# Conv state, conv weights and last conv inputs moved by rows and turned on chip, and w_out's split tied behind the newest scores

## The chip, the core and the metric

The kernel runs on one core of a Trainium2 chip. A core has TensorE (PE in the profile; PEld is its weight load), VectorE (DVE), ScalarE (ACT), GpSimd (POOL) and SyncE (SP), each with a queue of its own that it works through in order. In this kernel SP issues all transfers; they run on 16 DMA engines. The metric is the device time of one execution in microseconds (us), the median of several runs.

## The reference

One step of a one-layer streaming encoder, in float32. For the prompt (2048 tokens of 1024) and a sample of 32 tokens:

```
u  = rmsnorm(h, g_pre_mix);  z = u @ w_in      # columns B | C | X | Q | K | V, 512 each
zp = concat(hist, C * X)                       # hist: 0 for the prompt, state_conv for the sample
y  = b_conv + sum(zp[:, j:j+t] * w_conv[j] for j in 0..2);   conv_out = zp[:, -2:]
a  = differential attention of 4 heads on Q, K, V (two softmax maps, chunk mask, rmsnorm with g_subln)
h  = h + rmsnorm(concat(B * y, a) @ w_out)
h  = h + rmsnorm(relu(rmsnorm(h) @ w_up)^2 @ w_down)
h  = h + rmsnorm((p @ w_pe) * sigmoid(h @ w_g))
```

It returns h, k and v of both parts, and `conv_out` of both, the last two columns of C * X: `conv_prompt` and `conv_sample`, 2 x 512 values each. `state_conv` is 2 x 512, `w_conv` 3 x 512, `b_conv` 512, `g_subln` 128.

## The kernel before

All matrix products run on PE in float16 pairs: a float32 operand is split into a high half (ACT, L170) and a low half (DVE, L105) by `split`, and three products are added. Features lie on the 128 partitions in the conv and the projections, so the 512 conv channels are 4 groups (j, one for each head) of 128 partitions.

Start (L740 to L852, about 0 to 85 us). SP loads the x tiles, the gain and the first weight tiles of w_in. `hist` (state_conv) is loaded behind x tile 1 (L744), `wcv`, `bcv` and `gsa` (w_conv, b_conv, g_subln) in `small_loads` (L757 to L759); each reads a vector of DRAM into 128 partitions, so that one packet carries one value. The order of PE, ACT and DVE is written out by hand here (`manual_schedule`, L782): x tile 0 is normed and turned, `warm(11)` puts 11 matmuls on PE, then the second weight tile is prepared and the first projections run.

Attention part (about 85 to 945 us). For each head j a unit is 128 queries: `scores` (L596) puts matmuls on PE and, for each 512 columns, one DVE step (L610) that adds the bias and takes the running maximum; POOL negates the maximum (L100), ACT takes the exponential (L617). `turn` and `values` follow for the units before it. Between these steps `weave` (L1066) puts pieces of a second list of work, `between(j)` (L1029): the projections of the next head, and the conv of this one as three chunks, C, X and B. `c_group` (L429) evacuates C into `cz`, one buffer of 2 + 2048 columns, whose first two are 0 (in `czs`, for the sample, they are a POOL copy of `hist`, L434). `x_group` multiplies X into it. `b_group` (L446) forms y on POOL and DVE, multiplies with B and stores it to `mixc_d` (L461); on the sample's turn it stores the last two columns of `cz` and `czs` to the outputs (L463, L464), one pair for each head, one value in each packet. The buffer of y (tag kvo, three of them) is shared with the k and v outputs. The buffer of `cz` is taken over by `sample_attention` (L513). Each weight tile of w_in takes five steps: load (L256), maximum on DVE (L140), two small steps through PE, split.

In head 3 `w_out_load` (L875) loads the eight row blocks of w_out and takes their maxima (L891), `w_out_scales` makes the scales, and from unit 9 on the second list is `early` (L1018): `w_out_split` (L917) splits the eight blocks, one for each step of the list, and `mix_tile` runs the first two tiles of the output projection. From about 945 us on follow the output projection, the MLP and the gate, bound by PE.

Outside `manual_schedule` a planner puts each engine's instructions in order when the kernel is built: it runs its own estimate of the time, and an instruction that is ready goes ahead of earlier ones that aren't. `issue_after(ins)` makes the planner keep each instruction of a block that runs on the engine of `ins` behind `ins`.

Of the kernel before, what the change touches and what calls it, by code (L numbers as in the profile page):

```python
# [9 lines left out]
F32 = mybir.dt.float32  # L10
# [7 lines left out]
P = 128  # L18
D = 1024
FT = D // P  # L20
S = 2048
NTG = 4
TG = 512
NH = 4
DS = 32
# [4 lines left out]
BIG = 3.0e38  # L30
# [4 lines left out]
def hymba_step_kernel(  # L35
# [192 lines left out]
    mconv = cst.tile([P, NH * (NTG + 1)], F32, name="mconv")  # L228
    nlam = cst.tile([P, 1], F32, name="nlam")
    alam = cst.tile([P, 1], F32, name="alam")  # L230
    wcv = cst.tile([P, 3, NH], F32, name="wcv")
    bcv = cst.tile([P, NH], F32, name="bcv")
    hist = cst.tile([P, 2, NH], F32, name="hist")
    gsa = cst.tile([P, 1], F32, name="gsa")
    gain = {}

# [209 lines left out]
    def b_group(c, tg, parts=1):  # L446
        j = c.j
        n = TG if tg < NTG else DS
        z = cz[0][:, tg * TG:tg * TG + TG + 2] if tg < NTG else cz[1]
        yt = misc.tile([P, TG], F32, tag="kvo", bufs=3, name="yt")  # L450
        y = yt[:, :n]
        ts(G, y, z[:, 0:n], wcv[:, 0, j:j + 1], MUL, bcv[:, j:j + 1], ADD)
        stt(y, z[:, 1:n + 1], wcv[:, 1, j:j + 1], y, MUL, ADD)
        stt(y, z[:, 2:n + 2], wcv[:, 2, j:j + 1], y, MUL, ADD)
        ps = yield from proj_fm(c.w, tg, parts)
        o = y if tg < NTG else mix_s[:, j, :]
        stt(o, ps, c.iw, y, MUL, MUL)
        k = j * (NTG + 1) + tg
        V.tensor_reduce(out=mconv[:, k:k + 1], in_=o, op=MAX, axis=AX.X, apply_absolute_value=True)
        if tg < NTG:  # L460
            st(out=mixc_d[j, :, cols(tg)], in_=o)  # L461
        else:
            st(out=conv_prompt[0, 0][:, j * P:(j + 1) * P].rearrange("w p -> p w"), in_=cz[0][:, S:S + 2])  # L463
            st(out=conv_sample[0, 0][:, j * P:(j + 1) * P].rearrange("w p -> p w"), in_=cz[1][:, DS:DS + 2])  # L464

    GROUP = {GK: k_group, GV: v_group, GC: c_group, GX: x_group, GB: b_group}

# [114 lines left out]
    class Unit:  # L582
# [13 lines left out]
        def scores(self):  # L596
            h, nk, qb = heads[self.j], self.nk, self.qb
            qs, q = h[("qs", qb // 4)], slice(qb % 4 * P, (qb % 4 + 1) * P)
            self.s, self.z = [], []
            for m in range(2):  # L600
                s_ = att.tile([P, S], F32, tag="s", bufs=4, name=f"s{m}")
                prev = None
                for c0, w_ in self.chunks:
                    ps = psc.tile([P, TG], F32, tag="sc", bufs=3, name="sc")
                    kc = h["ks"][m][:, c0:c0 + w_]
                    T.matmul(ps[:, :w_], qs[:, 2 * m, q], kc, start=True, stop=False)
                    T.matmul(ps[:, :w_], qs[:, 2 * m + 1, q], kc, start=False, stop=True)  # L607
                    mx = t1("mx")
                    b0 = S - nk + c0
                    V.tensor_tensor_reduce(out=s_[:, c0:c0 + w_], in0=ps[:, :w_], in1=bias[:, b0:b0 + w_],  # L610
                                           scale=h["idd"], scalar=-BIG if prev is None else prev,
                                           op0=ADD, op1=MAX, accum_out=mx)
                    prev = mx
                    if c0 + w_ == nk:
                        nm, zz = t1("nm"), t1(f"z{m}")
                        ts(G, nm, prev, -1.0, MUL)
                        A.activation(out=s_[:, :nk], in_=s_[:, :nk], func=AF.Exp, bias=nm, accum_out=zz)  # L617
                        self.s.append(s_)
                        self.z.append(zz)
                    yield  # L620
# [88 lines left out]
    with tc.tile_pool(name="p1", bufs=1, side="right") as p1:  # L709
# [30 lines left out]
        ld(out=g1, in_=g_pre_mix[0].partition_broadcast(P))  # L740
        order[1].step()
        loaded += [load_x(1)]
        for w in range(2):
            ld(out=hist[:, w, :], in_=state_conv[0, 0][w].rearrange("(t p) -> p t", p=P))  # L744
        loaded += [load_x(t) for t in range(2, 7)]

        def small_loads():
            ldx = ld
            lam = []
            for i, (a_, b_) in enumerate(((lambda_q1, lambda_k1), (lambda_q2, lambda_k2))):  # L750
                la = p1.tile([P, 64], F32, tag=f"la{i}", name="la")
                lb = p1.tile([P, 64], F32, tag=f"lb{i}", name="lb")
                ldx(out=la, in_=a_[0].partition_broadcast(P))
                ldx(out=lb, in_=b_[0].partition_broadcast(P))
                lam.append((la, lb))
            for w in range(3):
                ldx(out=wcv[:, w, :], in_=w_conv[0][w].rearrange("(t p) -> p t", p=P))  # L757
            ldx(out=bcv, in_=b_conv[0].rearrange("(t p) -> p t", p=P))
            ldx(out=gsa, in_=g_subln[0].rearrange("(p o) -> p o", o=1))  # L759
            yield  # L760
            le = []
            for la, lb in lam:
                V.tensor_tensor(out=la, in0=la, in1=lb, op=MUL)
                sm_, ex = t1("lsum"), t1("lexp")
                V.tensor_reduce(out=sm_, in_=la, op=ADD, axis=AX.X)
                A.activation(out=ex, in_=sm_, func=AF.Exp)
                le.append(ex)
            V.tensor_tensor(out=nlam, in0=le[1], in1=le[0], op=SUB)
            ts(V, nlam, nlam, -0.2, ADD)
            absval(alam, nlam)  # L770

            ts(V, gsa, gsa, 0.8, MUL)
            gs, _, sa, gain["isa"] = scaled_gain(p1, g_subln[0], "g3", 10)
            gain["sa"] = sa
            ts(V, gsa, gsa, sa, MUL)
# [6 lines left out]
        with tc.manual_schedule(engines={ET.PE, ET.Activation, ET.DVE}):  # L782
            first, second = order[0], order[1]

            def summed(t):
                rs[t] = sum_x(*loaded[t])

            def normed(t):
                norm_x(*loaded[t], rs[t])

            def turned(t):
                turn_x(t, *loaded[t])

            def warm(n):

                for _ in range(n):
                    T.matmul(smb[:, :P], ident, ident, start=True, stop=True)

            warm(12)
            summed(0)  # L800
            first.step()
            first.step()
            normed(0)
            first.step()
            summed(1)
            norm_by_pool(loaded[1][0], rs[1])
            _, gain["su"], gain["isu"] = gain_scale(g1, "g1", 9)
            first.step()
            turned(0)
            warm(11)  # L810
            second.step()
            summed(2)
            groups = [c_group(first, 0, 4), x_group(second, 0, 4)]
            next(groups[0])
            second.step()
            normed(2)
            second.step()
            turned(1)
            second.step()
            nxt["k"] = 2  # L820
            summed(3)
            next(groups[0])
            next(groups[1])
            turned(2)
            normed(3)
            next(groups[1])
            summed(4)
            for t in range(2, NT):

                if len(loaded) < NT:  # L830
                    loaded.append(load_x(len(loaded)))
                if t + 2 < NT:
                    normed(t + 2)
                if t + 1 < NT:
                    turned(t + 1)
                if t + 3 < NT:
                    summed(t + 3)
                if t % 4 == 0:
                    groups = [g(c, t // 4, 4 if t < S // P else 1) for g, c in ((c_group, first), (x_group, second))]
                for g in groups:  # L840
                    next(g, None)
                if t % 4 == 3 or t == NT - 1:
                    for g in groups:
                        all_of(g)
                if t in (2, 6):
                    next(later, None)
                if 5 < t < 14:
                    prepare(3)
                if t >= 14 and order[4].done < 4:
                    prepare(4)  # L850
# [66 lines left out]
    def w_out_split():  # L917

        s_put.close()
        here["small2"] = ctx.enter_context(tc.tile_pool(name="sml2", bufs=4, reuse_waits="tile"))  # L920
        pwo = s_wo.enter_context(tc.tile_pool(name="pwo", bufs=1, reuse_waits="tile"))
        here["ppost"] = s_wo.enter_context(tc.tile_pool(name="ppost", bufs=1, reuse_waits="tile"))
        for r in ROWS:
            w = wo[r] = pwo.tile([P, 2, D], F16, tag="w", bufs=8, name="w")
            split(w[:, 0], w[:, 1], out_scale["sgs"][r], out_scale["aswo" if r < 4 else "swo"])
            yield


# [907 lines left out]
```

## Time and profile before

| | us |
|---|---|
| median of 3 runs (2559.03 to 2565.12) | 2562.55 |
| the profiled execution | 2561.83 |
| its span, first to last instruction | 2560.1 |
| PE busy in the span | 2464.4 (96%) |
| DVE, ACT, POOL busy | 1691.2, 1138.2, 747.8 |
| mean granted clock of TensorE | 0.986 of full speed |
| elements stored by L463 and L464, to landing | 9.9 in the middle |

The page divides the span into busy time of each engine. Busy time alone doesn't say what a change is worth; that is read from the views of single stretches: an engine's timeline (when each instruction started, how long it took, how long the engine stood idle before it and for what), the view of who waited for whom, windows with the busy time of every engine, and the list of transfers with their time from issue to landing. TensorE's granted clock is 1.00 at 2.4 GHz and 0.50 at 1.2 GHz; a value between them is a mean over a stretch.

### The profile page before, as it was taken

How to read it: one execution, taken by the hardware profiler on the slowest of the kernel's cores; microseconds unless marked ns; L12 is line 12 of the kernel's file. 1: busy time of each engine (PE TensorE's matmuls, PEld its weight loads, DVE VectorE, ACT ScalarE, POOL GpSimd, SP SyncE). 2: the span in 40 equal slices, each digit the busy share in tenths (PEclk: the TensorE clock that was granted, in tenths of full speed). 3: DMA queues.
4: the chain of work that ended last, by engine and by line, in shares of the span. 5: the costliest groups of instructions: out<-in, count | busy, mean ns of one | idle time of the engine just before them, and what ended most of it. 6: DMA issues, size and time to landing. Idle time of an engine off the chain costs nothing.

```text
span 2560.1 us, 41714 instructions
## 1 busy us (share of the span) xinstructions
PE 2464.4 (96%) x15979; PEld 1286.8 (50%) x15979; DVE 1691.2 (66%) x2930; ACT 1138.2 (44%) x1976; POOL 747.8 (29%) x1299
## 2 busy tenths in 40 slices
PE   8999999998999789999999999999999999999998
PEld 7756654754754445444444444444444444444444
DVE  6578968957988857865656656645455447645664
ACT  5436635634653645544434434444233322424553
POOL 2143344333333333423223222210121102323442
PEclk9999999999999799999999999999999999999999
DMA  5134534523553334554454454366554547531221
GB/s 179 51 83 95 109 68 93 118 50 85 120 113 83 88 122 154 179 214 153 153 181 156 149 181 141 136 228 231 185 203 140 177 155 240 202 108 59 79 83 54
DMA packets 350489, 345.35 MB, mean 135 GB/s; under 512 B 155920, under 2 KB 246448, under 8 KB 350288
## 3 DMA queue, kind: packets, MB, share of 16 engines
q1 hardware_dynamic: 350288, 342.68, 44.5%
q8 instruction: 125, 2.05, 0.3%
q14 instruction: 76, 0.62, 0.1%
HBM read 206.68 MB, written 97.92 MB: 119 GB/s over the span
## 4 chain that ended last, share of the span: by engine, by line
PE 64%; DVE 5%; DMA 3%; issue 2%; POOL 1%; ACT 1%; DVEq 0%; SPq 0%; POOLq 0%; ACTq 0%
PE mm L1368 8%; PE mm L1370 7%; PE mm L1369 7%; PE mm L1599 6%; PE mm L1601 6%; PE mm L1600 6%; PE mm L944 5%; PE mm L946 5%; PE mm L948 5%; DVE s L105 1%; PE lin L313 1%; PE lin L314 1%; PE lin L315 1%; DVE s L610 1%; PE ptr L185 1%
## 5 line engine op out<-in xcount | busy, mean ns | idle before, releaser
L1601 PE MATMUL mm<-v,hl 128*128 128x512 f16 x896 | 341.0, 381 | 4.4 <-DVE hl L1561 4.3
L1599 PE MATMUL mm<-v,hl 128*128 128x512 f16 x896 | 340.8, 381 | 3.8 <-ACT hl L1560 3.4
L1600 PE MATMUL mm<-v,hl 128*128 128x512 f16 x896 | 341.4, 381 | 0.0
L313 PE MATMUL lin<-uh,whl 128*128 128x512 f16 (+1 forms) x832 | 264.4, 333 | 16.9 <-DVE yt L105 14.0
L314 PE MATMUL lin<-ul,whl 128*128 128x512 f16 (+1 forms) x832 | 264.9, 333 | 1.4 <-DVE ul L105 1.3
L315 PE MATMUL lin<-uh,whl 128*128 128x512 f16 (+1 forms) x832 | 264.3, 333 | 0.2 <-DVE whl L105 0.2
L1561 DVE TENSOR_TENSOR hl<-fr,hl 128x1024 f16<-128x1024 f32 x112 | 147.5, 1326 | 174.4 <-ACT hl L1560 171.7
L1560 ACT ACTIVATE hl<-fr 128x1024 f16<-128x1024 f32 x112 | 116.9, 1051 | 303.7 <-PE mm L1601 290.5
L617 ACT ACTIVATE s<-s,nm 128x128 f32<-128x128 f32 (+15 forms) x128 | 153.6, 1200 | 167.9 <-POOL nm L100 167.3
L1368 PE MATMUL mm<-u,w 128*128 128x512 f16 x448 | 169.8, 379 | 1.1 <-ACT w L170 1.1
L1369 PE MATMUL mm<-u,w 128*128 128x512 f16 x448 | 169.8, 379 | 0.0
L1369 PE MATMUL mm<-u2b,w 128*128 128x512 f16 x448 | 169.8, 379 | 0.0
L1368 PE MATMUL mm<-u2b,w 128*128 128x512 f16 x448 | 169.2, 380 | 0.1
L1370 PE MATMUL mm<-u,w 128*128 128x512 f16 x448 | 168.9, 379 | 0.0
L1370 PE MATMUL mm<-u2b,w 128*128 128x512 f16 x448 | 168.5, 379 | 0.0
L1599 PEld LDWEIGHTS <-hl 128*128 128x128 f16 x896 | 88.0, 98 | 114.1 <-issue 7.7
L610 DVE CUSTOM_DVE_ANT_0 s<-sc,bias,mx 128x512 f32<-128x512 f32 (+3 forms) x192 | 134.9, 702 | 15.1 <-PE sc L607 10.5
L1601 PEld LDWEIGHTS <-hl 128*128 128x128 f16 x896 | 87.9, 98 | 113.2 <-DVE hl L1561 7.2
L1600 PEld LDWEIGHTS <-hl 128*128 128x128 f16 x896 | 88.0, 98 | 105.2 <-issue 2.6
L1370 PEld LDWEIGHTS <-w 128*128 128x128 f16 x896 | 87.6, 98 | 105.3
L1368 PEld LDWEIGHTS <-w 128*128 128x128 f16 x896 | 88.7, 99 | 100.2 <-ACT w L170 1.2
L1369 PEld LDWEIGHTS <-w 128*128 128x128 f16 x896 | 87.6, 98 | 98.7 <-issue 0.3
(456 smaller groups left out, 5844.4 us busy)
## 6 DMA issues: line engine op xcount, KB each, us to landing
ff_d<-e SPq DMA_DIRECT2D x224, 256.0 KB, 2.1
fr<-ff_d SPq DMA_DIRECT2D x112, 512.0 KB, 4.4
raw<-in_w_down_dram SPq DMA_DIRECT2D x80, 512.0 KB, 4.7
xt<-in_x_prompt_dram SPq DMA_DIRECT2D x32, 512.0 KB, 4.4
stg<-in_w_up_dram SPq DMA_DIRECT2D x16, 1024.0 KB, 6.5
stgd<-in_w_down_dram SPq DMA_DIRECT2D x16, 1024.0 KB, 5.4
stg<-in_w_in_dram SPq DMA_DIRECT2D x24, 512.0 KB, 3.9
h_d<-ht SPq DMA_DIRECT2D x16, 512.0 KB, 2.9
```

The lines of the kernel that those rows point to most:

```text
L313: T.matmul(o, w[:, 0, ft], rh[:, ft, c], start=(ft == 0), stop=False)
L314: T.matmul(o, w[:, 0, ft], rl[:, ft, c], start=False, stop=False)
L315: T.matmul(o, w[:, 1, ft], rh[:, ft, c], start=False, stop=(ft == FT - 1))
L610: V.tensor_tensor_reduce(out=s_[:, c0:c0 + w_], in0=ps[:, :w_], in1=bias[:, b0:b0 + w_], scale=h["idd"], scalar=-BIG if prev is None else ...
L617: A.activation(out=s_[:, :nk], in_=s_[:, :nk], func=AF.Exp, bias=nm, accum_out=zz)
L1368: T.matmul(o, w[:, c, 0, kt], x[:, :, 0, kt], start=first and kt == 0, stop=False, skip_group_check=True)
L1369: T.matmul(o, w[:, c, 0, kt], x[:, :, 1, kt], start=False, stop=False, skip_group_check=True)
L1370: T.matmul(o, w[:, c, 1, kt], x[:, :, 0, kt], start=False, stop=kt == 3, skip_group_check=True)
L1561: V.tensor_tensor(out=hl[:, 1], in0=fr, in1=hl[:, 0], op=SUB)
L1599: T.matmul(ps, hl[:, 0, u % 2, c], v[:, 0], start=(u == 0), stop=False)
L1600: T.matmul(ps, hl[:, 0, u % 2, c], v[:, 1], start=False, stop=False)
L1601: T.matmul(ps, hl[:, 1, u % 2, c], v[:, 0], start=False, stop=(u == NU - 1))
```

## The change

The 25 rows of 128 values that the conv and the norm need (8 of state_conv, 12 of w_conv, 4 of b_conv, 1 of g_subln) are loaded as rows into one tile `rows_` behind x tile 1. After `warm(11)` one PE transpose turns it, and a DVE copy puts it into `few`; `hist`, `wcv` and `bcv` are views of `few`, and `gsa` is made from its last column. The loads in `small_loads` are gone.

In each head two POOL copies put the last two columns of `cz` and `czs` into `ends`. In head 3 one PE transpose turns `ends` (16 columns) into 16 rows, ACT copies them out of PSUM, and two stores write 8 rows of 512 B each.

`scores` notes its newest DVE step in `here["ev"]`, and each block's split in `w_out_split` is put behind it by `issue_after`; as that step is DVE's, it binds the low half and not ACT's high half.

```diff
+    few = cst.tile([P, 25], F32, name="few")
+    hist = few[:, 0:8].rearrange("p (w t) -> p w t", t=NH)
+    wcv = few[:, 8:20].rearrange("p (w t) -> p w t", t=NH)
+    bcv = few[:, 20:24]
+    ends = cst.tile([P, 2, 2, NH], F32, name="ends")
...
-            st(out=conv_prompt[0, 0][:, j * P:(j + 1) * P].rearrange("w p -> p w"), in_=cz[0][:, S:S + 2])
-            st(out=conv_sample[0, 0][:, j * P:(j + 1) * P].rearrange("w p -> p w"), in_=cz[1][:, DS:DS + 2])
+            G.tensor_copy(ends[:, 0, :, j], cz[0][:, S:S + 2])
+            G.tensor_copy(ends[:, 1, :, j], cz[1][:, DS:DS + 2])
+            if j == NH - 1:
+                pt = ptp.tile([P, TG], F32, tag="tp", name="pte")
+                T.transpose(pt[:16, :P], ends.rearrange("p a w t -> p (a w t)"), ident)
+                eo = misc.tile([P, TG], F32, tag="kvo", bufs=3, name="eo")
+                A.copy(eo[:16, :P], pt[:16, :P])
+                for a_, o_ in ((0, conv_prompt), (8, conv_sample)):
+                    st(out=o_[0, 0].rearrange("w (t p) -> (w t) p", p=P), in_=eo[a_:a_ + 8, :P])
...
+                    here["ev"] = getattr(ev, "ins", ev)
...
-        for w in range(2):
-            ld(out=hist[:, w, :], in_=state_conv[0, 0][w].rearrange("(t p) -> p t", p=P))
+        rows_ = p1.tile([25, P], F32, name="rows")
+        for a_, n_, i_ in ((0, 8, state_conv[0, 0]), (8, 20, w_conv[0])):
+            ld(out=rows_[a_:n_], in_=i_.rearrange("w (t p) -> (w t) p", p=P))
+        ld(out=rows_[20:24], in_=b_conv[0].rearrange("(t p) -> t p", p=P))
+        ld(out=rows_[24:25], in_=g_subln[0].rearrange("(o p) -> o p", o=1))
...
-            for w in range(3):
-                ldx(out=wcv[:, w, :], in_=w_conv[0][w].rearrange("(t p) -> p t", p=P))
-            ldx(out=bcv, in_=b_conv[0].rearrange("(t p) -> p t", p=P))
-            ldx(out=gsa, in_=g_subln[0].rearrange("(p o) -> p o", o=1))
...
-            ts(V, gsa, gsa, 0.8, MUL)
+            ts(V, gsa, few[:, 24:25], 0.8, MUL)
...
             warm(11)
+            pt = ptp.tile([P, TG], F32, tag="tp", name="ptf")
+            T.transpose(pt[:, :25], rows_, ident[:25, :25])
+            V.tensor_copy(few, pt[:, :25])
             second.step()
...
-            split(w[:, 0], w[:, 1], out_scale["sgs"][r], out_scale["aswo" if r < 4 else "swo"])
+            with tc.issue_after(here["ev"]):
+                split(w[:, 0], w[:, 1], out_scale["sgs"][r], out_scale["aswo" if r < 4 else "swo"])
```

## Rows read from the trace of the kernel before

**Rows 1.** The page: busy us of PE in the span.
```profile
PE 2464.4 (96%) x15979; PEld 1286.8 (50%) x15979; DVE 1691.2 (66%) x2930; ACT 1138.2 (44%) x1976; POOL 747.8 (29%) x1299
```
**Rows 2.** Windows: length, busy us (instructions) of PE, PEld, DVE, ACT, POOL, clock, DMA, GB/s.
```profile
960.00:2160.00 1200.00, 1197.66 (x6467) 550.90 (x6465) 719.84 (x927) 486.04 (x760) 263.65 (x253) 1.00 0.52 176
840.00:880.00 40.00, 22.25 (x146) 15.14 (x145) 36.64 (x88) 25.15 (x43) 17.84 (x40) 0.70 0.43 105
880.00:905.00 25.00, 22.98 (x162) 13.71 (x161) 19.21 (x45) 17.78 (x42) 13.43 (x38) 1.00 0.28 83
584.72:595.70 10.98, 10.97 (x57) 5.29 (x57) 9.19 (x24) 2.84 (x7) 3.78 (x10) 0.83 0.43 114
```
**Rows 3.** Who waited for whom, PE, 0 to 960 us: total, times, longest.
```profile
PE lin L313 <- DVE yt L105: 14.0, 4, 7.9
```
**Rows 4.** The list of transfers: count, KB each, median us from issue to landing.
```profile
stg<-in_w_in_dram SPq DMA_DIRECT2D x24, 512.0 KB, 3.9
mixc_d<-yt SPq DMA_DIRECT2D x16, 256.0 KB, 2.5
out_dram<-cz SPq DMA_DIRECT2D x4, 1.0 KB, 9.9
out_dram<-kt SPq DMA_DIRECT2D x4, 16.0 KB, 1.6
```
**Rows 5.** Timelines, head 2: start, us, engine, line, operation [idle before, releaser].
```profile
566.68 0.39 SPq L256 DMA_DIRECT2D stg<-in_w_in_dram  x1
567.16 0.53 SPq L464 DMA_DIRECT2D out_dram<-czs  x1
581.60 1.22 DVE L140 TENSOR_REDUCE am<-stg 128x1 f32<-128x1024 f32 x1 [12.06 <-DMA stg<-in_w_in_dram]
584.72 0.58 PE L313 MATMUL lin<-uh,whl 128*128 128x512 f16 x1 [7.88 <-DVE yt L105]
```
**Rows 6.** Timelines, head 1.
```profile
364.72 0.44 SPq L464 DMA_DIRECT2D out_dram<-czs  x1
369.07 0.34 SPq L461 DMA_DIRECT2D mixc_d<-yt  x1
376.77 0.77 POOL L102 TENSOR_SCALAR yt<-cz,wcv,bcv 128x512 f32<-128x512 f32 x1 [6.84 <-DMA mixc_d<-yt]
381.39 0.38 PE L606 MATMUL sc<-ks,qs 128*128 128x512 f16 x1 [3.08 <-DVE mx L610]
```
**Rows 7.** Timelines, head 3.
```profile
795.77 0.81 SPq L888 DMA_DIRECT2D wst<-in_w_out_dram  x2
796.85 0.40 SPq L463 DMA_DIRECT2D out_dram<-cz  x1
806.58 1.22 DVE L891 TENSOR_REDUCE wmax<-wst 128x1 f32<-128x1024 f32 x1 [5.76 <-DMA wst<-in_w_out_dram]
811.14 0.38 PE L313 MATMUL lin<-uh,whl 128*128 128x512 f16 x1 [1.74 <-DVE yt L105]
```
**Rows 8.** Timelines, w_out's split in head 3.
```profile
861.97 4.86 DVE L105 SCALAR_TENSOR_TENSOR w<-wst,aswo,w 128x1024 f16<-128x1024 f32 x4
863.55 0.26 ACT L507 ACTIVATE jko<-smb 128x128 f16<-128x128 f32 x1
859.70 0.38 PE L606 MATMUL sc<-ks,qs 128*128 128x512 f16 x1 [2.90 <-DVE mx L610]
868.46 0.26 PE L655 MATMUL smb<-vhl,at 128*128 128x128 f16 x1 [8.17 <-DVE yg L100]
```
**Rows 9.** Timelines, the start: the state's loads, their POOL copy, the first projection.
```profile
4.45 2.02 SPq L744 DMA_DIRECT2D hist<-in_state_conv_dram  x2
12.82 0.19 POOL L434 COPY czs<-hist 128x2 f32<-128x2 f32 x1 [6.45 <-DMA hist<-in_state_conv_dram]
17.48 0.22 PE L314 MATMUL lin<-ul,whl 128*128 128x128 f16 x1 [1.33 <-DVE ul L105]
```
**Rows 10.** Timeline of POOL, head 1: a step on one column.
```profile
359.13 2.28 POOL L102 TENSOR_SCALAR kk<-sg,z,k 128x1 f32<-128x1 f32 x1
```

More of the change, by code (lines that the diff above doesn't have):

```diff
@@ L230, in hymba_step_kernel @@
     alam = cst.tile([P, 1], F32, name="alam")
-    wcv = cst.tile([P, 3, NH], F32, name="wcv")
-    bcv = cst.tile([P, NH], F32, name="bcv")
-    hist = cst.tile([P, 2, NH], F32, name="hist")
+    few = cst.tile([P, 25], F32, name="few")
[3 more added lines that the diff above has]
+    ends = cst.tile([P, 2, 2, NH], F32, name="ends")
     gsa = cst.tile([P, 1], F32, name="gsa")
@@ L609, in scores @@
                     b0 = S - nk + c0
-                    V.tensor_tensor_reduce(out=s_[:, c0:c0 + w_], in0=ps[:, :w_], in1=bias[:, b0:b0 + w_],
-                                           scale=h["idd"], scalar=-BIG if prev is None else prev,
-                                           op0=ADD, op1=MAX, accum_out=mx)
+                    ev = V.tensor_tensor_reduce(out=s_[:, c0:c0 + w_], in0=ps[:, :w_], in1=bias[:, b0:b0 + w_],
+                                                scale=h["idd"], scalar=-BIG if prev is None else prev,
+                                                op0=ADD, op1=MAX, accum_out=mx)
+                    here["ev"] = getattr(ev, "ins", ev)
                     prev = mx
```

## The prediction

> **What bounds the kernel now.** I read the busy times first: TensorE (PE) is busy 2464.4 us of a span of 2560.1 [rows 1], so a change is worth what it takes out of the other 96 us, and out of the time in which PE runs at half clock. Windows of 20 us over the whole span show where those lie: before 960 us, in the start and in the attention part, and at the very end; from 960 to 2160 us PE is busy 1197.66 of 1200 [rows 2]. So I went through the attention part with the view of who waited for whom. One line stands out: the projection matmul L313 waits for the conv's evacuation on VectorE (DVE) four times, 14.0 us together, 7.9 the longest [rows 3]. All four lie in the conv stretches of heads 2 and 3. What DVE was waiting for there is seen in its timeline. At 581.6 us it has stood 12.06 us for a weight tile from DRAM [rows 5]; at 806.6 us 5.76 us for a row block of w_out [rows 7]. In head 1 GpSimd (POOL) stands 6.84 us for a store of mixc_d, whose buffer it wants back [rows 6]. The list of transfers gives what such ones usually take: 3.9 us for a tile of 512 KB, 2.5 for the store [rows 4]. The weight tile took 581.60 - 566.68 = 14.9. What the three places share is in the queue of SyncE (SP): beside each of the late transfers stand the two stores of the conv state, L463 and L464 [rows 5 to 7], 1 KB each, with 9.9 us to landing, against 1.6 for a 16 KB store that moves whole rows [rows 4].
>
> The stretch after that is bound by DVE: from 840 to 880 us DVE is busy 36.64 of 40 us, PE only 22.25, at a mean granted clock of 0.70; from 880 to 905 DVE is busy 19.21 of 25 [rows 2]. The low halves of w_out's split stand there in clumps, the last four as one piece of 4.86 us [rows 8].
>
> **The conv state's stores.** The change takes the eight stores out of the four heads, and puts one pair of row stores behind a transpose at the end of head 3. What goes with them is the lateness of their neighbours.
>
> Head 2: the tile issued at 566.68 lands at about 570.6 instead of 581.6, so DVE's work moves up by 11.0 us. PE had other matmuls until 576.8, then stood 7.88 us [rows 5], and came back at half clock: in the 10.98 us from 584.72 its mean granted clock was 0.83, which is 10.98 * 0.17 = 1.9 us lost [rows 2]. PE's own loss is 9.8, DVE's 11.0; with PE the nearer bound I take **10**. If another wait follows behind it, half: 5.
>
> Head 1: the store issued at 369.07 would land at 371.6 and POOL's step start there instead of at 376.77, 5.2 us earlier; PE lost only 3.08 [rows 6]. I take **3**, with 0 and 5.2 as ends.
>
> Head 3: the second w_out block of 795.77 would land near 800.5, where DVE gets free from its other work, instead of 806.58: 5.8 us for DVE. PE's direct loss behind it is 1.74 [rows 7]; later waits may belong to it or not. I take **4**, between 1.7 and 5.8. In head 0 I found no wait beside the stores, and take 0.
>
> Here a rule speaks against the last term. The row: this load was issued at 795.77, ahead of the store at 796.85 [rows 7], and was late all the same. The Trainium skill, DMA: Bandwidth & Descriptors, section Queues, rings and completion order, says that a DMA engine's semaphore increment lands only after every earlier write of that engine. Taken by the word, a load ahead of the store has nothing to wait for, head 3's term falls away, and the sum below is 4 smaller. The row and the rule part; I go by the row, since nothing else stands beside that load in the queue.
>
> **The inputs.** Two loads of state_conv and five of w_conv, b_conv and g_subln, one element per packet, become four loads of 8, 12, 4 and 1 rows into `rows_`. SP issued the two old ones in 2.02 us [rows 9]; four issues at 0.4 to 0.5, as others take in these rows, are 1.6 to 2.0: nothing, and the five later issues disappear from a stretch in which nobody waits for SP. The data are wanted by a transpose that stands behind the 11 warm-up matmuls. On PE the second matmul behind them waits until 17.48 for DVE's `ul` anyway [rows 9], and the transpose's PSUM buffer is freed by the same `ul`; the state has landed by 12.8 already in the old form [rows 9]. What is added on this path is one transpose and one DVE copy of 25 columns, 0.2 us each by the neighbours: **-0.4**. The POOL copy of `hist` now comes after about 18 us instead of 12.8; if it stands ahead of the norm of tile 1 in POOL's queue, it costs up to 1.4. A gain has room too: ScalarE stood for x tile 1, but that was issued before the old loads, so I count none.
>
> **New steps at the heads.** Eight POOL copies of two columns, 0.19 us each in the nearest row [rows 9], one transpose of 16 rows and one ScalarE copy, each below 0.3: **-0.3**. POOL takes its work in order, and behind a copy that waits for the conv's DVE step stand the negated maxima on which ScalarE's exponentials wait. The buffer of `cz`, which the sample's attention takes over, is released by those copies and no longer by a store of 9.9 us. The two row stores of 4 KB are near the 16 KB row with 1.6 us [rows 4], and nobody waits for them before the end.
>
> **The tie of w_out's split.** The instructions stay the same; DVE's low halves (8 of about 1.24 us) may not pass the newest scores traced before them. Today four of them go ahead of the scores and of `yg`, while PE stands 8.17 us [rows 8]. ScalarE's high halves aren't tied: the square that `yg` needs starts behind them at 863.55 [rows 8], so `yg` could start at about 864.6 rather than 868.07, 3.5 us earlier. Upper end: the whole wait, 8.2. Lower end: the 9.9 us of halves fall into 880 to 905, where DVE has 5.8 us free [rows 2]; 4.1 are left over, a loss. I take **4**, as the 3.5 is read from rows and the rest needs the planner.
>
> **The sum.** 10 + 3 + 4 + 4 - 0.4 - 0.3 = 20.3 us. The profiled execution took 2561.83 (span 2560.1 and 1.7 around it), 0.7 below the median of the runs shown. That gives 2541.5; against the median 2542.2. I say **2542**. From 960 us on PE is the bound, so what is gained before that stays.
>
> **The rivals.** (1) **Part is given back**: the planner orders every queue anew, and in place of a late transfer PE meets the next chain; half of the three conv terms and nothing of the tie, 8.5 - 0.7 = 7.8, is 2554. For it speaks that DVE has little air after 840 us, against it that in heads 1 and 2 DVE and POOL were idle while they waited. (2) **The stores were not the cause**: the late transfers stay late for another reason, and the time stays at 2562. Against it: the 24 weight tiles take 3.9 in the middle [rows 4], and the one of 14.9 is the one between two such stores.
>
> (3) **POOL is held by DVE.** A POOL step on one column took 2.28 us while DVE went through three long instructions [rows 10]. If all eight copies meet that, and the exponentials wait behind each, it is 8 * 2.1 = 16.7 us, which leaves 2559. The Trainium skill, SBUF — State Buffer, section Who interferes with whom, states that of DVE and GpSimd the second one to ask for their shared port is blocked until the first is done; by that rule each copy would pay what is left of a DVE instruction. The rows here have POOL steps of that size at both 0.2 and 2.3 us, and PE has matmuls beside most, so the chance is small.
>
> (4) **Lockstep, the slower side.** PE's queue is in order too. If the first mix tile's matmuls stay in front of the scores, each of the eight rows waits for a tied half, which waits for a score, which waits for PE: one round per row. A score round was 2.9 us where PE waited for one at 859.7 [rows 8]. Eight are 23 us, against 16.3 gained elsewhere: 2569. It decides from 16.3 / 8 = 2.0 us per row on. Against it: the planner knows the tie and has scores and products to put between.
>
> **How the numbers follow.** Forecast, 2536 to 2549: 0.55. Better than that, the upper ends together (11 + 5.2 + 5.8 + 8.2 - 0.7 = 29.5, 2532): 0.07. Rival 1, 2549 to 2557: 0.20. Rival 2: 0.06; rival 3: 0.05. Rival 4: 0.07. A measurement of this kernel can tell about 0.2%, 5.1 us, from no change. So faster is 0.55 + 0.07 + 0.20 = 0.82, same 0.06 + 0.05 = 0.11, slower 0.07. The range 2533 to 2556 leaves out rivals 2 to 4 and the outer edges of the first two, 2 in 10.
>
> **What would show it.** Right, if the weight tile of head 2's stretch lands in about 4 us, DVE's wait for it falls from 12 to 1, PE's 7.9 us wait is gone and no half-clock stretch follows; if POOL's wait for mixc_d and DVE's for the second w_out block fall below 1; if w's halves stand singly between scores and PE's 8.2 us wait is halved. Wrong, if transfers of 10 us stay without those stores; if the copies into `ends` have POOL idle before them and exponentials late behind; if PE waits for `w` in the first mix tile; or if PE starts its first projection later than 17.9 us.

## The result and the profile after

| | before | after |
|---|---|---|
| median, us | 2561.51 (2559.03 to 2565.12) | 2534.59 (2532.97 to 2537.78) |
| ratio | | 0.9893, interval 0.9879 to 0.9907 |
| span of the profiled execution, us | 2560.1 | 2531.6 |

The change takes 26.9 us off the median; the forecast was 2542, that is 20, with a range of 2533 to 2556. The time is inside the range and 7 us better than the forecast. The first line is the page's busy line of the kernel after, to set beside [rows 1]; the second is the windows view from 960 us on, beside [rows 2] (columns as there).

```profile
PE 2456.3 (97%) x15981; PEld 1283.6 (51%) x15981; DVE 1692.4 (67%) x2931; ACT 1139.1 (45%) x1977; POOL 756.0 (30%) x1307
960.00:2160.00 1200.00, 1195.66 (x6461) 547.87 (x6460) 716.96 (x917) 478.34 (x737) 261.56 (x240) 1.00 0.52 177
```

PE is busy 8.1 us less (its mean granted clock is 0.991 instead of 0.986), and its idle time fell from 95.7 us to 75.3, most of it before 960 us. Which waits went is seen when the rows of the three heads are read again in the kernel after. Its line numbers have moved: the projection L313 is L317 here, L606 is L617, L610 is L621, L655 is L667, L944 is L959.

Head 2: the weight tile's issue on SP, DVE's step on it, PE's first projection behind it (timelines), all of PE's waits for `yt` before 960 us (who waited for whom), and the window from 580 to 600 us.

```profile
563.44 0.38 SPq L260 DMA_DIRECT2D stg<-in_w_in_dram  x1
567.14 1.22 DVE L140 TENSOR_REDUCE am<-stg 128x1 f32<-128x1024 f32 x1 [0.80 <-DMA stg<-in_w_in_dram]
583.17 0.38 PE L317 MATMUL lin<-uh,whl 128*128 128x512 f16 x1 [1.04 <-DVE yt L105]
PE lin L317 <- DVE yt L105: 1.3, 2, 1.0
580.00:600.00 20.00, 18.96 (x149) 10.62 (x147) 17.83 (x47) 8.61 (x16) 10.99 (x27) 1.00 0.33 85
```

The tile is there 567.14 - 563.44 = 3.7 us after its issue, where it took 14.9 [rows 5]; DVE's wait fell from 12.06 to 0.80, PE's from 7.88 to 1.04, the 14.0 us of such waits [rows 3] to 1.3, and the clock is 1.00 where it was 0.83 [rows 2]. Head 1 and head 3, timelines:

```profile
362.51 0.19 POOL L468 COPY ends<-czs 128x2 f32<-128x2 f32 x1 [0.64 <-DVE czs L105]
370.75 0.77 POOL L102 TENSOR_SCALAR yt<-cz,few 128x512 f32<-128x512 f32 x1 [1.75 <-DMA mixc_d<-yt]
783.05 1.22 DVE L905 TENSOR_REDUCE wmax<-wst 128x1 f32<-128x1024 f32 x1 [0.68 <-DMA wst<-in_w_out_dram]
807.91 0.38 PE L317 MATMUL lin<-uh,whl 128*128 128x512 f16 x1 [0.30 <-DVE yt L105]
```

POOL's wait for the store of mixc_d is 1.75 instead of 6.84 [rows 6]; the prediction had asked for less than 1. DVE's wait for w_out is 0.68 where it was 5.76, and PE's 0.30 where it was 1.74 [rows 7]. Now the split of w_out (timelines, then PE's wait in the first mix tile):

```profile
835.31 4.25 ACT L170 ACTIVATE w<-wst,aswo 128x1024 f16<-128x1024 f32 x4
839.47 0.26 ACT L518 ACTIVATE jko<-smb 128x128 f16<-128x128 f32 x1
840.46 0.75 DVE L105 SCALAR_TENSOR_TENSOR s<-s,sg,s 128x512 f16<-128x512 f32 x1 [5.62 <-ACT s L170]
841.53 0.27 PE L667 MATMUL smb<-vhl,at 128*128 128x128 f16 x1 [6.04 <-DVE yg L100]
874.69 1.03 PE L959 MATMUL mm<-w,mx 128*128 128x512 f16 x2 [2.88 <-DMA mx<-ya_d]
```

DVE no longer has four low halves there as one piece; it stands idle 5.62 us behind ScalarE, whose high halves aren't tied. PE's wait is 6.04 instead of 8.17 [rows 8], not halved as the prediction asked, and a new one of 2.88 us stands 33 us later, for `mx`, the first mix tile's input read back from DRAM. Whether the tie gained anything is a question for the runs below.

### The profile page after: what moved, and what is told of

Same layout as the page of the kernel before. It is cut to its first block, busy times and chain, and to the rows that moved or that the text cites. A ratio compares the mean times of both kernels' runs of the same rounds, so it can differ in the third digit from the quotient of the medians.

```text
span 2531.6 us, 41709 instructions
## 1 busy us (share of the span) xinstructions
PE 2456.3 (97%) x15981; PEld 1283.6 (51%) x15981; DVE 1692.4 (67%) x2931; ACT 1139.1 (45%) x1977; POOL 756.0 (30%) x1307
## 4 chain that ended last, share of the span: by engine, by line
PE 79%; DVE 9%; DMA 5%; ACT 3%; issue 3%; POOL 2%; SPq 0%; DVEq 0%; POOLq 0%; ACTq 0%
PE mm L1383 8%; PE mm L1385 8%; PE mm L1384 8%; PE mm L1614 7%; PE mm L1616 7%; PE mm L1615 7%; PE mm L959 4%; PE mm L961 4%; PE mm L963 4%; PE lin L317 4%; PE lin L318 4%; PE lin L319 4%; DVE s L105 2%; DVE s L621 2%; PE sc L617 1%
## 5 line engine op out<-in xcount | busy, mean ns | idle before, releaser
L317 PE MATMUL lin<-uh,whl 128*128 128x512 f16 (+1 forms) x832 | 261.6, 330 | 4.1 <-DVE yt L105 1.3
L319 PE MATMUL lin<-uh,whl 128*128 128x512 f16 (+1 forms) x832 | 261.7, 330 | 0.7 <-DVE whl L105 0.7
L621 DVE CUSTOM_DVE_ANT_0 s<-sc,bias,mx 128x512 f32<-128x512 f32 (+3 forms) x192 | 134.9, 702 | 16.0 <-PE sc L618 11.8
```

The lines of the kernel that those rows point to most:

```text
L317: T.matmul(o, w[:, 0, ft], rh[:, ft, c], start=(ft == 0), stop=False)
L319: T.matmul(o, w[:, 1, ft], rh[:, ft, c], start=False, stop=(ft == FT - 1))
L621: ev = V.tensor_tensor_reduce(out=s_[:, c0:c0 + w_], in0=ps[:, :w_], in1=bias[:, b0:b0 + w_], scale=h["idd"], scalar=-BIG if prev is None ...
```

## The experiments

My theory after the result: the stores, element by element, kept their neighbours in the DMA engines waiting; taking them out is the whole gain, and the other parts lie within a few us of nothing. The rivals: the tie or the loads carry a part (by single traces about 4 to 5 us for the tie and 1 for the loads), and, for the stores, that what was harmful is the number of one-value packets rather than that they are written. Times in us are worked out from the ratio and the median of the kernel before that ran beside them.

### The parts alone

`e1_tie` is the kernel before with these lines of the diff alone:

```
+                    ev = V.tensor_tensor_reduce(out=s_[:, c0:c0 + w_], ...)
+                    here["ev"] = getattr(ev, "ins", ev)
...
+            with tc.issue_after(here["ev"]):
                 split(w[:, 0], w[:, 1], ...)
```

> The kernel before with the tie alone; the conv state's stores and the loads stay one element per packet. Theory (each part has its own price): DVE's 4.86 us clump of low halves is gone, PE's wait of 8.17 us for yg shrinks to about 4 to 6 because ScalarE's high halves still stand ahead of the square that yg needs, and the time falls by 4 to 5 us, to about 2557. Rival (the gain is the planner's, any edit sets off a new order): the time moves by 10 us or more, or not at all. Rival (the tie is the main part): 15 us or more.

Measured 2567.46 against 2562.26; ratio 1.0016 (1.0004 to 1.0027), 4.1 us slower (1.0 to 6.9). The gain that was expected isn't there.

`e2_stores` is the kernel before with the copies into `ends`, the transpose and the two row stores in place of L463 and L464, and nothing else.

> The kernel before with the conv state's last columns kept on chip and stored by rows at the end of head 3; no tie, the loads as before. Theory: this carries most of the gain. By the shift of matching matmuls between the two traces it is 4.4 us in head 1, 11.1 in head 2, 6.9 in head 3, together 22, so about 2539; DVE's wait of 12.06 us for the weight tile falls to about 1. Rival (planner): far from the sum of its parts, above 2550.

Measured 2539.15; ratio 0.9905 (0.9890 to 0.9920), a gain of 24.3 us (20.5 to 28.2). That is nearly the whole change, as expected.

`e3_loads` is the kernel before with the row loads into `rows_`, their transpose and `few`, and nothing else.

> The kernel before with the inputs alone loaded by rows and turned on PE; stores and split as before. Theory: x tile 1 is squared 0.9 us earlier (11.5 us instead of 12.4) since the old loads of the state no longer stand beside its transfer; 1 us or less, the same by the clock of several runs, about 2561. Rival: these loads were a cost for other transfers as the stores were, 5 us or more.

Measured 2565.30; ratio 1.0010 (1.0001 to 1.0020), 2.6 us slower (0.3 to 5.1): no gain by itself.

`e4_no_tie` is the kernel after with `split` untied again.

> The changed kernel without the tie: stores and loads by rows, the split of w_out left to the planner. Theory: the tie's 5 us are lost again, about 2539, and DVE's low halves stand in a clump ahead of yg as in the kernel before. Rival (without the late transfers the split's clump costs nothing): as the changed kernel, 2534.

Measured 2538.28; ratio 0.9896 (0.9879 to 0.9914). The interval holds the kernel after's 0.9893, so what the tie does in company of the stores couldn't be told from this; it was taken up again below.

### One head at a time

`e5_head2` and `e6_head3` are the kernel before with one head's stores by rows:

```
+            if j != 2:          # e6_head3: 3
                 st(out=conv_prompt[0, 0][:, j * P:(j + 1) * P].rearrange("w p -> p w"), ...)
                 st(out=conv_sample[0, 0][:, j * P:(j + 1) * P].rearrange("w p -> p w"), ...)
+            else:
+                G.tensor_copy(ends[:, 0, :, j], cz[0][:, S:S + 2])
+                G.tensor_copy(ends[:, 1, :, j], cz[1][:, DS:DS + 2])
```

> The kernel before with one part of the change: head 2's ends of the convolution go by rows, those of heads 0, 1 and 3 element by element as before; element-wise loads at the start and the split as before. Theory (the 512 one-value packets of a head's two stores keep the next small DMAs of the core waiting): only the stretch around 580 us closes, by the 11 us that the changed kernel gained there, so about 2551 us against 2562, with head 1's and head 3's waits as in the kernel before. Rival (the stretch was set by something else that the change moved): 2562. Rival (the gain is handed back at head 3, whose stores meet a later load): 2556 or more.

> As the run before, but head 3's ends alone go by rows; heads 0, 1 and 2 as in the kernel before. The two kernels' traces give 6.9 us to this stretch, so about 2555 us. [...]

`e5_head2` took 2551.79 against 2565.86; ratio 0.9944 (0.9929 to 0.9958), a gain of 14.4 us (10.8 to 18.2). `e6_head3` took 2559.10; ratio 0.9978 (0.9968 to 0.9987), a gain of 5.6 us (3.3 to 8.2). Both agree with what was expected, taken as a gain (the kernel before took 4 us more beside these runs than in the first result). Heads 0 and 1 are left with 24.3 - 14.4 - 5.6 = 4.3, an estimate only, as each of the three has an interval of 5 to 8 us. Timelines of `e5_head2`: DVE's step on the weight tile in head 2, PE's wait, and what is late in head 3.

```profile
574.91 1.22 DVE L140 TENSOR_REDUCE am<-stg 128x1 f32<-128x1024 f32 x1 [0.85 <-DMA stg<-in_w_in_dram]
591.14 0.38 PE L314 MATMUL lin<-uh,whl 128*128 128x512 f16 x1 [1.32 <-DVE yt L105]
801.65 0.77 POOL L102 TENSOR_SCALAR yt<-cz,wcv,bcv 128x512 f32<-128x512 f32 x1 [5.69 <-DMA mixc_d<-yt]
```

The wait of head 2 closes and nothing else does. In head 3, whose stores are the old ones here, it is now mixc_d that is late and not w_out: which transfer suffers depends on what stands next to the stores, not on the transfer. Timelines of `e6_head3`: head 2 as before, head 3 free.

```profile
585.86 1.22 DVE L140 TENSOR_REDUCE am<-stg 128x1 f32<-128x1024 f32 x1 [11.50 <-DMA stg<-in_w_in_dram]
588.98 0.58 PE L314 MATMUL lin<-uh,whl 128*128 128x512 f16 x1 [7.82 <-DVE yt L105]
802.41 1.22 DVE L903 TENSOR_REDUCE wmax<-wst 128x1 f32<-128x1024 f32 x1 [0.15 <-DMA wst<-in_w_out_dram]
```

The load of w_out was issued ahead of the store [rows 7] and is on time as soon as the store behind it is gone: 0.15 us of waiting where it was 5.76.

### Writes or packets, one store or two

`e7_reads` is the kernel after with as many one-value packets as the old stores had, at their place, but as loads. It reads two columns per head into a tile that nothing uses:

```
+            for i_ in range(2):
+                G.tensor_copy(dum[:, i_], (cz[0][:, S:S + 2], cz[1][:, DS:DS + 2])[i_])
+                ld(out=dum[:, i_], in_=state_conv[0, 0][:, j * P:(j + 1) * P].rearrange("w p -> p w"))
```

> The changed kernel with two loads of 256 one-value packets each added per head, at the place where the removed stores stood (they read the convolution state into a tile that nothing reads). The number and size of packets is then that of the kernel before, only their direction is turned. If the packets themselves (their number at 4 bytes each) made the waits: about 2556, with the waits at 364, 567 and 797 us back. If it was the writing to DRAM: about 2535, as the changed kernel. In between: both count.

Measured 2540.31 against 2565.86; ratio 0.9902 (0.9888 to 0.9917), a gain of 25.1 us (21.3 to 28.7). So nearly the whole gain stays: that they are written to DRAM counts, not how many packets there are. The lists of transfers around head 2 (count, KB each, median us from issue to landing), first of the kernel before from 560 to 600 us, then of `e7_reads` from 555 to 600:

```profile
stg<-in_w_in_dram SPq DMA_DIRECT2D x1, 512.0 KB, 14.9
out_dram<-cz SPq DMA_DIRECT2D x1, 1.0 KB, 10.0
out_dram<-czs SPq DMA_DIRECT2D x1, 1.0 KB, 16.8
```

```profile
stg<-in_w_in_dram SPq DMA_DIRECT2D x2, 512.0 KB, 4.0
dum<-in_state_conv_dram SPq DMA_DIRECT2D x2, 1.0 KB, 4.5
```

256 values of 4 bytes land after 4.5 us when they are read from DRAM (the trace has the landing of one of the two loads), after 10.0 when they are written. In this head the two writes land one behind the other: with the issues at 564.41 and 567.16 they land at 574.4 and 584.0, 9.6 us apart. The load between them, issued at 566.68 [rows 5], lands at 581.6. It isn't so in heads 1 and 3, where the two stores are issued 0.6 and 0.9 us apart: there they land together, within 0.2 us. Lists of transfers of the kernel before, first the stores of head 1, then those of head 3 with the second block of w_out ahead of them:

```profile
out_dram<-cz SPq DMA_DIRECT2D x1, 1.0 KB, 11.1
out_dram<-czs SPq DMA_DIRECT2D x1, 1.0 KB, 10.7
```

```profile
wst<-in_w_out_dram SPq DMA_DIRECT2D x1, 512.0 KB, 10.4
out_dram<-cz SPq DMA_DIRECT2D x1, 1.0 KB, 9.9
out_dram<-czs SPq DMA_DIRECT2D x1, 1.0 KB, 9.2
```

What the DMA engines move meanwhile stands in windows (columns as in [rows 2]): of the kernel before in head 2, of `e7_reads` at the same place, and twice of the kernel before in head 3.

```profile
568.00:576.00 8.00, 8.00 (x38) 3.60 (x37) 0.66 (x4) 0.90 (x2) 1.50 (x5) 1.00 0.42 30
```

```profile
563.00:567.00 4.00, 4.00 (x20) 1.83 (x19) 1.99 (x7) 1.13 (x2) 2.12 (x9) 1.00 0.71 197
```

```profile
796.00:801.00 5.00, 5.00 (x38) 2.86 (x37) 4.66 (x11) 2.34 (x6) 1.40 (x4) 1.00 0.63 210
801.00:804.00 3.00, 3.00 (x16) 1.35 (x15) 0.00 (x0) 0.00 (x0) 0.00 (x0) 1.00 0.00 0
```

In head 2 the engines move 30 GB/s while the first write is on its way, against 197 in `e7_reads`: the tile itself is moved slowly. In head 3 it is different. By 801 us 210 GB/s times 5 us, 1.05 MB, have been moved, which is both blocks of w_out, and from 801 to 804 nothing moves; the second block still lands only at 806.6, 0.2 us before the first store. There the data weren't late, but the signal that they had landed was.

The Trainium skill, DMA: Bandwidth & Descriptors, section Specifications, says that below 512 B a DMA engine reads, modifies and writes. That fits the direction seen here: what is slow is writing single values. That each of the 256 packets did so, no row here shows.

`e12_half` is the kernel after with one of the two stores of each head, the prompt's, element by element again:

```
+            st(out=conv_prompt[0, 0][:, j * P:(j + 1) * P].rearrange("w p -> p w"), in_=cz[0][:, S:S + 2])
...
-                for a_, o_ in ((0, conv_prompt), (8, conv_sample)):
+                for a_, o_ in ((8, conv_sample),):
```

> The changed kernel with one of each head's two stores element by element again (the prompt's: 256 packets of one value), the sample's by rows. If the harm goes with the number of one-value packets written: half of what the rows gained, about 2548 us against 2536 for the changed kernel, with half of the 12 us wait for the next head's weights back. If one store is hidden by the slack that the two overran: 2538 or less. If the last packet to be written is what counts, whatever their number: 2555 or more.

Measured 2561.04 against 2562.53; ratio 0.9991 (0.9982 to 1.0000), a gain of 2.3 us (0 to 4.6). That is the last of the three outcomes written down: nearly all of the gain is gone. Timelines of `e12_half`: head 1, head 2 with the issues on SP, and head 3.

```profile
377.65 0.77 POOL L102 TENSOR_SCALAR yt<-cz,few 128x512 f32<-128x512 f32 x1 [8.66 <-DMA mixc_d<-yt]
567.09 0.53 SPq L468 DMA_DIRECT2D out_dram<-cz  x1
569.36 0.39 SPq L260 DMA_DIRECT2D stg<-in_w_in_dram  x1
581.23 1.22 DVE L140 TENSOR_REDUCE am<-stg 128x1 f32<-128x1024 f32 x1 [8.97 <-DMA stg<-in_w_in_dram]
804.73 1.22 DVE L906 TENSOR_REDUCE wmax<-wst 128x1 f32<-128x1024 f32 x1 [5.83 <-DMA wst<-in_w_out_dram]
```

All three neighbours are late again, by 8.66, 8.97 and 5.83 us of waiting where two stores made 6.84, 12.06 and 5.76 [rows 5 to 7]. One store of this kind stands beside each of them and is enough: a load issued 2.3 us behind it takes 581.23 - 569.36 = 11.9 us. So the harm doesn't halve with the packets: it goes by the neighbours met. In heads 1 and 3 that fits two stores landing together in the time of one; in head 2, where they land one behind the other, the tile took 14.9 us with two and 11.9 with one.

### What the tie and the loads are worth

Four kernels on one chip in more rounds: the kernel after (`e9_after_again`), the same without the tie (`e11_no_tie_again`, as `e4_no_tie`), the kernel before with the stores by rows and the tie but the old loads (`e10_stores_tie`), and the kernel after with ScalarE's halves tied too (`e8_act_tie`):

```
+                        ex = A.activation(out=s_[:, :nk], ..., func=AF.Exp, bias=nm, accum_out=zz)
+                        here["ex"] = getattr(ex, "ins", ex)
...
+            with tc.issue_after(here["ev"]), tc.issue_after(here["ex"]):
```

> The changed kernel itself once more, in more rounds, on the same chip as the three runs beside it, to tell a few us apart: 0.9893 of the kernel before, as it was.

> The changed kernel without the tie, again, in more rounds. The traces give the tie 3.9 us at the first normalised output behind the split and 4 us at the end. If that is the tie's: 4 us over the changed kernel beside it (0.9909 of the kernel before). If it is the scatter of executions: the same time as the changed kernel.

> The kernel before with stores by rows and the tie, but with the element-wise loads at the start. If the row loads at the start are worth 0.9 us, as the first stretch of the traces says: 1 us over the changed kernel. If they lose the 0.4 us of the prediction: 0.4 us under it. Both lie near the changed kernel; a time 4 us off would mean that the loads matter later than in the first stretch.

> The changed kernel with one thing more: ScalarE's half of each row of the split is tied behind the newest exponential as VectorE's is tied behind the newest scores. In the changed kernel's trace ScalarE makes eight halves in one stretch (4.25 us for the last four) and the normalised output waits for it, 6.0 us on TensorE. Theory (that stretch is what is left of the wait): the 6.0 us shrink to about 2, and the time falls by 3 to 4 us. Rival (the halves only move on and are waited for by the next heads or by the first matmuls with w): no change or a few us more, as with the tie alone.

| against 2563.45 | median, us | ratio | interval |
|---|---|---|---|
| e9_after_again | 2536.80 | 0.9888 | 0.9873 to 0.9903 |
| e11_no_tie_again | 2535.96 | 0.9893 | 0.9876 to 0.9909 |
| e10_stores_tie | 2542.14 | 0.9911 | 0.9896 to 0.9925 |
| e8_act_tie | 2536.18 | 0.9889 | 0.9874 to 0.9904 |

With and without the tie the medians differ by 0.8 us, where each interval is some 8 us wide: the tie is worth nothing that these runs can tell. Tying ScalarE's halves too brings nothing, so no version here is shown to beat the kernel after.

Where the tie's gain goes is seen when one stretch is measured by its own ends: from the `yg` ahead of the split over the next `yg` to the first matmul on `u`, where the next stage begins. Timelines, three rows of `e11_no_tie_again` and three of the kernel after:

```profile
826.14 0.35 DVE L100 TENSOR_SCALAR yg<-smb,rso 128x128 f32<-128x128 f32 x1 [0.23 <-PE pty L712]
843.22 0.35 DVE L100 TENSOR_SCALAR yg<-smb,rso 128x128 f32<-128x128 f32 x1
1061.57 0.38 PE L1381 MATMUL mm<-u,w 128*128 128x512 f16 x1
```

```profile
827.92 0.35 DVE L100 TENSOR_SCALAR yg<-smb,rso 128x128 f32<-128x128 f32 x1 [0.23 <-PE pty L713]
841.13 0.35 DVE L100 TENSOR_SCALAR yg<-smb,rso 128x128 f32<-128x128 f32 x1
1065.39 0.38 PE L1383 MATMUL mm<-u,w 128*128 128x512 f16 x1
```

To the next `yg` it is 17.1 us untied and 13.2 tied: 3.9 gained. To the next stage it is 235.4 untied and 237.5 tied: nothing left. The other traces say the same. The first step takes 16.7 to 17.1 in the seven kernels without the tie and 13.2 to 14.4 in the six with only the low halves tied; the whole stretch takes 235.4 to 239.7 in the first and 235.9 to 241.0 in the others. The windows of 10 us tell where it is given back (columns as in [rows 2]; first `e11_no_tie_again`, then the kernel after, at 10 and at 40 us from the first `yg`):

```profile
836.14:846.14 10.00, 2.91 (x26) 2.52 (x25) 9.99 (x16) 4.54 (x9) 7.18 (x7) 0.50 0.16 30
866.14:876.14 10.00, 7.45 (x59) 4.74 (x57) 8.26 (x22) 6.90 (x18) 4.94 (x15) 1.00 0.46 131
```

```profile
837.92:847.92 10.00, 5.28 (x36) 3.90 (x36) 6.98 (x16) 7.61 (x16) 4.39 (x10) 0.57 0.33 65
867.92:877.92 10.00, 6.43 (x43) 3.65 (x42) 9.21 (x23) 8.10 (x21) 7.49 (x20) 0.79 0.59 176
```

In the first pair PE gains 2.4 us of work by the tie. In the second it loses 1.0, and its clock falls from 1.00 to 0.79: the wait of 2.88 us for `mx` stands there, and PE comes back from it at the lower clock; in the next window it is busy all 10 us, but at 0.87, where without the tie it is 1.00. Twenty us later the kernel after has one more window that isn't full, at 9.0 of 10 us. Its second trace (`e9_after_again`) has the wait for `mx` too, 2.67 us. In `e1_tie`, with late stores ahead of it, two rows of who waited for whom (820 to 960 us) show the same pair, the wait for `yg` and the new one:

```profile
PE smb L656 <- DVE yg L100: 13.6, 4, 8.2
PE mm L946 <- DMA mx<-ya_d: 3.2, 1, 3.2
```

`e8_act_tie` shows it once more, further on: PE's waits for `yg` are down to 2.0 us in two, the next `yg` comes after 6.8 us, and the stretch to the next stage still takes 236.5, with the waits now at the scores. Two rows of the same view:

```profile
PE sc L617 <- DVE mx L621: 9.8, 8, 3.5
PE smb L668 <- DVE yg L100: 2.0, 2, 1.3
```

As to the loads: the second `yg` of the whole run, near 174 us, comes at 174.12 to 176.09 in the six kernels with the old loads and at 173.74 to 174.69 in the eight with the new ones, on the mean 174.9 and 173.9: about 1 us gained at the start. The times alone (`e10_stores_tie` 5.3 us over `e9_after_again`, `e3_loads` 2.6 over the kernel before) don't agree in sign. The 5.3 is what was written down as a sign that the loads matter later than at the start, but the intervals of the two overlap, so that stays open; I read the loads as no more than a few us either way.

## Why the prediction was right, and where its sum was not

The sign, the mechanism and the range held. The sum of 20.3 is short by 7 of the 26.9, and two of its terms were off in opposite directions.

**Head 2: 10 predicted, 14.4 by `e5_head2` (10.8 to 18.2).** The mechanism is shown: the tile on time, the 12 us wait and the half clock gone, all as the last part of the prediction asked. The size was short because I took one of PE's two waits in this stretch: the view that I showed counted four waits for `yt`, 14.0 together [rows 3], I priced the one of 7.88, and left out a second one of 2.26 us at 597.96, in the same conv stretch. With it the term is 12. The traces agree: against the kernel before, PE's matching matmuls in `e5_head2` stand 4.0 us later at 560 us and 8.5 us earlier at 600, 12.5 in all.

**Head 1: 3 predicted, 4.4 by the two traces**, 5.4 us of shift at PE's work around 410 us, less 0.9 from the start. From 460 us on only 3.7 us of the shift are left, so 1.7 were given back (in `e2_stores` 4.4 stay); by the runs 4.3 is left for heads 0 and 1. The 4.4 lies inside 0 to 5.2. The profiled execution of before was a mild case: POOL's wait was 6.84 us in it [rows 6], and 7.07 to 9.04 in the five kernels of the experiments that left head 1's stores as they were or kept one of them.

**Head 3: 4 predicted, 5.6 by `e6_head3` (3.3 to 8.2)**, the upper end of my bounds. The rule of the Trainium skill that I weighed against it, DMA: Bandwidth & Descriptors, section Queues, rings and completion order, speaks of the writes that came earlier; that a store behind a load can't hold it up is what I read into it. The run decides: without the store behind it the load is on time. The windows above show what was late, the signal and not the data. That fits the rule if on some of the engines the store's writes came ahead of the load's signal; on which engine a packet ran isn't in these views, so this stays open. And the row of 795.77 holds two issues [rows 7]: the late block is the second, issued at 796.2, 0.65 us ahead of the store and not 1.

**The inputs: -0.4 predicted, about +1 by the traces, not settled by the runs** (`e3_loads` 2.6 us slower, `e10_stores_tie` 5.3 over `e9_after_again`). By the traces the step that failed is "I count none" for x tile 1. ScalarE's first pass over that tile starts at 11.54 us instead of 12.40, so in these traces the load does land earlier, though it is issued ahead of the small loads that were replaced; and the transpose meets the wait for `ul` and costs 0.2. The POOL copy did come later, at 18.82 instead of 12.82, and delayed nobody.

**The new steps: -0.3 predicted.** The eight POOL copies take 2.5 us together, mostly 0.19 us each (groups of POOL's instructions below); one of them took 1.1, why isn't shown. PE's transpose takes 0.27. No wait behind them shows, so rival 3, POOL held by DVE, didn't come.

```profile
L468 POOL COPY ends<-czs 128x2 f32<-128x2 f32 x4 | 1.7, 424 | 1.8 <-DVE czs L105 1.8
L467 POOL COPY ends<-cz 128x2 f32<-128x2 f32 x4 | 0.8, 191 | 7.8 <-DVE cz L105 7.8
```

**The tie: 4 predicted, none measured.** The step itself was right: ScalarE's untied halves now set `yg`, and `yg` comes 3.9 us sooner where I had 3.5. What failed is that I booked a shorter wait in the middle of a stage as time gained at its end, without asking what is late next. The answer stood in the prediction as the mechanism of rival 1, "PE meets the next chain", which is what happened to this one term and, but for the 1.7 us of head 1, not to the conv terms. By itself the tie was even 4.1 us slower in `e1_tie`; why more than nothing is lost there I can't say.

**The slower side.** Rival 4, lockstep, didn't come: the low halves stand in ones, twos and threes between scores (not singly, as the prediction asked), and PE doesn't wait for each of them. Rival 2 is refuted by `e5_head2` and `e6_head3`.

**Added up again:** 24.3 for the stores, 1 for the inputs (by the traces), 0 for the tie make 25.3, against 26.9 measured (23.8 to 31.0 by the interval of the ratio). So the total came out near the forecast because the stores brought 7 more than their 17 and the tie 4 less. That the two misses partly cancelled is luck: with the tie's 4 us on top the time would have been about 2531, better than the range.

One thing nearly misled me. The traces of before and after end 28.5 us apart, and about 5 us of that lie behind the split, as if the tie had given them. But from the first matmul on `u` to the end the fourteen traces take 1466.2 to 1472.3 us, and the 1466.2 is that of the kernel after; its second trace, in `e9_after_again`, has 1471.4. The same kernel scatters by 5 us there, and the part of the shift that can be put down to the change is the 23.5 us that have come together at the `yg` ahead of the split (851.39 in before, 827.92 in after).

## What to carry to other kernels

A store that scatters single values to DRAM is priced by what stands beside it in the DMA queue, not by its 1 KB: turn the values on chip and store rows, and turn all of them, for one such store left next to a load that somebody waits for gives the harm back. Add up every wait of a stretch, not only the longest, before pricing what removes its cause. And measure a reordering between two fixed points that enclose the stage: a wait that is shorter inside it is a gain only when the next stage starts earlier, and in more than one trace.

## What the runs showed of the hardware

- Writing 256 single values of 4 bytes to DRAM took 7.9 to 11.1 us to landing in seven of the eight stores of the kernel before, and 16.8 in the eighth, issued while another was on its way. Reading as many took 2.0 and 4.5 us in the two landings that the trace of `e7_reads` has; at the crowded start two loads of 512 single values took 8.1 and 7.6.
- Two such writes issued 0.6 and 0.9 us apart landed within 0.2 us of each other; two issued 2.8 us apart, with a load between them, landed 9.6 us apart.
- Such a write delayed a load of 512 KB issued 2.3 us behind it by about 8 us (11.9 instead of 3.7), and one issued 0.65 us ahead of it took 10.4 us, where the load just ahead of that took 3.5. In the second case the data had been moved some 6 us before the landing was signalled. As many single-value loads, at about the same places, left 25.1 us of the gain.
- One write beside a transfer cost nearly as much time as two (2.3 us of the gain left out of 27). Why such a write takes so long, and from what packet size on it doesn't, no run here shows.
- After a wait of 2.88 us PE's window shows a granted clock of 0.79, in a stretch where the kernel without that wait has 1.00; the next window, busy throughout, shows 0.87. So an idle PE can cost more than the idle time.
